# Three load buffers for VectorE's adaLN pieces, with RQ and bt moved into the `mt` ring

## The chip, the cores and the metric

The kernel runs on one core of a Trainium2 chip. The metric is the device time of one execution in microseconds. The engines are TensorE (PE: matmuls, with PEld for its weight loads), VectorE (DVE), ScalarE (ACT), GpSimd (POOL) and SyncE (SP). POOL and SP here mostly issue DMAs.

## The reference: what is computed

Two layers of a diffusion block work on 256 context tokens and 256 latent tokens of width 2048. Each layer makes the adaLN rows (shift, scale, gate) from a conditioning vector, normalises and modulates the tokens, projects them with one wide matrix, runs three mixers on parts of the columns (S5, attention, a bidirectional mLSTM) and projects back. Cut to what matters here:

```python
for layer in range(DEPTH):
    shift, scale, gate = split(silu(c) @ ada_w[layer] + ada_b[layer], 3)       # 2048 x 6144
    xn = rmsnorm(h_lat, norm_w[layer]) * (1 + scale) + shift
    (..., ml_q, ml_k, ml_v, ml_o, ml_g, ml_z) = split_sections(xn @ w_in[layer])
    ya = s5_branch(...); yb = attention_branch(...)
    # mlstm: q, k = silu(depthwise conv of width 3); gates i, f from ml_g
    #   b = cumsum(log_sigmoid(f)); log_d = b_t - b_s + i_s; running max, exp
    yc = mlstm_branch(...)
    h_lat = h_lat + gate * (concat(ya, yb, yc) @ w_out[layer])
```

The context tokens go through the same layers with a conditioning vector of their own.

## The kernel before

All weights are streamed from HBM in chunks of 512 KB (128 x 1024). `wchunk` loads one into `raw` (three buffers, SP's queue); ScalarE rounds it to `hi`, VectorE subtracts to get `lo` (two buffers each). `proj_a` makes one output of 128 channels by 512 tokens in a PSUM tile `pa` from two chunks: 48 matmuls (`hi` by `xh`, `hi` by `xl`, `lo` by `xh`). `proj_b` does the same for outputs that have the tokens on partitions, in `pb`. Both draw on a pool of three PSUM banks, so the fourth `pa` needs the bank of the first. A callback reads the bank when it is full.

TensorE's stream of projections is the backbone of the program. Beside it, generators (`stream`) and the adaLN queue (`ada_step`) are advanced by `pump` after each chunk, at a rate given as a number. The Tile framework then puts each engine's instructions into one fixed order by its priorities and its account of buffers, so a change in buffers can move instructions on every engine.

The adaLN rows of layer 1 are not made on TensorE: VectorE makes them while the mLSTM part of a layer runs. `adv_open(pool, bufs, rate, ids)` opens a queue of pieces. `ada_load` issues the load of a piece (512 KB, from `adt`) on POOL's queue into an `ar` tile, of which there are `bufs`. `adv_piece` reduces a piece against a row tile `cb`: an instruction `aj` (L365) with a small read-out of its sum into `adp`. In layer 0 there are 64 pieces with two `aj` each (128 `aj`, rate ADR = 1.2 a chunk), in layer 1 there are 32 pieces with one each (rate 1.0). Ahead of the first piece `adv_rows` loads 1 MB into `cb` and applies silu in four steps: a tanh on ScalarE into an `mt` tile, L150 on it, and a product into `cb`.

`mt` is a ring of five tiles of 128 x 516 in the mLSTM pool, from which most short-lived tiles of this part are taken. One user is `ml_conv`, which follows each of the projections mk0 to mk3 and mq0 to mq3: ScalarE writes y from `pa` into an `mt` tile, two VectorE instructions (L153, `mt<-pa`) add the shifted taps out of `pa`, then tanh and a product give `mk`. After the second of them the bank is free.

`ml_gates` works on the input and forget gates as a stream, at the time of mk0 to mk3: `ga0` to `ga6` are small tiles for the logarithm of the sigmoid; `li` is a copy of the input gates; TensorE transposes to rows in PSUM (`psr`); VectorE makes `bt` (a cumulative sum, L1021), `RQ` (a difference, its running maximum L1023 and a copy L1024), and TensorE transposes `RQ` back into `psg`.

At the same time attention runs as another stream. For each head block VectorE reduces the scores (`sm`, L949), ScalarE takes the exponential (`g`), VectorE the reciprocal (L953), ScalarE scales `g`, and TensorE transposes it (`psP`) and multiplies by the values (`psO`). Later in the layer the stream `ml_chain` runs the mLSTM's chunk steps (`psm`, `G`, `hacc`) and `ml_final` its output (`psh`).

Of the kernel before, what the change touches and what calls it, by code (L numbers as in the profile page):

```python
# [9 lines left out]
F32 = mybir.dt.float32  # L10
# [35 lines left out]
ADR = 1.2  # L46
# [77 lines left out]
class Kern:  # L124
# [857 lines left out]
    def ml_gates(self, l):  # L982
        mp = self.mp
        GS = self.GS
        sm = lambda q: mp.tile([128, 4, 2, 4], F32, tag=f"ga{q}", bufs=1, name=self.nm("ga"))
        f, ab, y, u, ln, e = (sm(q) for q in range(6))
        self.V.tensor_copy(f, GS[:, :, :, 1])
        self.ts(ab, f, -1.0, OP.mult)
        self.tt(ab, ab, f, OP.max)
        self.act(y, ab, AF.Exp, scale=-1.0)  # L990
        self.ts(u, y, 1.0, OP.add)
        self.act(ln, u, AF.Ln)
        self.ts(e, u, -1.0, OP.add)
        self.tt(e, y, e, OP.subtract)
        self.V.reciprocal(u, u)
        self.tt(e, e, u, OP.mult)
        self.tt(ln, ln, e, OP.add)
        self.stt(f, f, 0.0, ln, OP.min, OP.subtract)
        li = mp.tile([128, 4, 2, 4], F32, tag="ga6", bufs=1, name=self.nm("ga"))
        self.V.tensor_copy(li, GS[:, :, :, 0])  # L1000
        yield
        rows = self.pA.tile([128, 512], F32, tag="bA", name=self.nm("psr"))
        for w, src in enumerate((li, f)):
            z = []
            for d in range(2):
                zt = mp.tile([128, 4, 2, 4], F32, tag=f"gz{w}{d}", bufs=1, name=self.nm("gz"))
                self.V.memset(zt, 0.0)
                if d == 0:
                    self.V.tensor_copy(zt[:, :, 0], src[:, :, 0])
                else:  # L1010
                    zv = zt.rearrange("p (a b) d h -> p a b d h", b=2)
                    sv = src.rearrange("p (a b) d h -> p a b d h", b=2)
                    self.V.tensor_copy(zv[:, :, 0, 1], sv[:, :, 1, 1])
                    self.V.tensor_copy(zv[:, :, 1, 1], sv[:, :, 0, 1])
                z.append(zt.rearrange("p a d h -> p (a d h)"))
            o = rows[:32, w * 128:w * 128 + 128]
            self.mm(o, z[0], self.c("I"), start=True, stop=False)
            self.mm(o, z[1], self.c("J"), start=False, stop=True)
        RQ = mp.tile([128, 128], F32, tag="RQ", bufs=1, name=self.nm("RQ"))
        bt = mp.tile([128, 128], F32, tag="bt", bufs=1, name=self.nm("bt"))  # L1020
        self.V.tensor_tensor_scan(bt[:32], self.c("ONE")[:32], rows[:32, 128:256], 0.0, op0=OP.mult, op1=OP.add)  # L1021
        self.tt(RQ[0:32], rows[:32, 0:128], bt[:32], OP.subtract)
        self.V.tensor_tensor_scan(RQ[32:64], RQ[0:32], RQ[0:32], -3.0e38, op0=OP.max, op1=OP.max)  # L1023
        self.V.tensor_copy(RQ[64:96], bt[:32])  # L1024
        yield
        pt = self.pA.tile([128, 512], F32, tag="bA", name=self.nm("psg"))
        self.tr(pt[:, 0:96], RQ[0:96], k=96)
        self.tr(pt[:, 128:224], RQ[0:96, 127:128].to_broadcast([96, 128]), k=96)
        TK = mp.tile([128, 12, 2, 4], F32, tag="TK", bufs=1, name=self.nm("TK"))
        self.V.tensor_copy(TK.rearrange("p a d h -> p (a d h)"), pt[:, 0:96])  # L1030
        LB = mp.tile([128, 3, 4, 8], F32, tag="LB", bufs=1, name=self.nm("LB"))
        self.V.tensor_copy(LB.rearrange("p a b c -> p (a b c)"), pt[:, 128:224])
        tr = mp.tile([128, 12, 4], F32, tag="tr", bufs=1, name=self.nm("tr"))
        self.V.tensor_copy(tr, TK[:, :, 1])
        yield
        pf = self.pA.tile([128, 512], F32, tag="bA", name=self.nm("psf"))
        self.mm(pf[:, 0:48], self.c("J"), tr.rearrange("p a h -> p (a h)"))
        self.V.tensor_copy(TK[:, :, 1], pf[:, 0:48].rearrange("p (a h) -> p a h", h=4))
        yield
        q = lambda n: TK[:, 4 * n:4 * n + 4].rearrange("p s d h -> p s (d h)")  # L1040
        a_, cm, b_ = q(0), q(1), q(2)
        t8 = lambda nme: mp.tile([128, 4, 8], F32, tag=nme, bufs=1, name=self.nm(nme))
        ms, ML, M, WIN, GU, W, DEC = (t8(n) for n in ("gms", "gML", "gM", "gWIN", "gGU", "gW", "gDEC"))
        self.V.memset(ms[:, 0], 0.0)
        for s in range(4):
            self.tt(ML[:, s], ms[:, s], LB[:, 1, s], OP.max)
            if s < 3:
                self.tt(ms[:, s + 1], LB[:, 2, s], ML[:, s], OP.add)
        self.tt(M, cm, ms, OP.max)
        self.tt(WIN, ms, M, OP.subtract)  # L1050
        self.act(WIN, WIN, AF.Exp)
        self.tt(GU, b_, M, OP.add)
        self.act(GU, GU, AF.Exp, scale=-1.0)
        self.tt(W, a_, ML, OP.subtract)
        self.act(W, W, AF.Exp)
        self.ts(W, W, 128.0 ** -0.5, OP.mult)
        self.tt(DEC, ms, ML, OP.subtract)
        self.act(DEC, DEC, AF.Exp)
        self.mg = dict(a=a_, M=M, WIN=WIN, GU=GU, W=W, DEC=DEC)
# [173 lines left out]
    def layer(self, l, sp):  # L1233
# [71 lines left out]
        mpg = tc.tile_pool(name=f"ml{l}", bufs=1, side="left", reuse_waits="tile")  # L1305
        mp = self.mp = mpg.__enter__()
        if need:
            self.adv_open(mp, 2, ADR, range(0, 64))
        else:
            self.adv_open(mp, 2, 1.0, range(64, 96))  # L1310
        self.msk = mp.tile([128, 2, 128], F32, tag="msk", bufs=1, name=self.nm("msk"))
        nc.sync.dma_start(self.msk.rearrange("p d t -> p (d t)"), self.i["mask"])
        self.ml_conv_w(l)
# [285 lines left out]
```

## Time and profile before

| | |
|---|---|
| median of 3 runs | 1673.41 us (1667.14 to 1675.38) |
| the profiled execution | 1667.69 us |
| its span | 1665.9 us |
| PE busy in it | 1588.9 us (95%) |
| DVE busy | 1203.8 us (72%) |
| ACT busy | 669.6 us (40%) |
| POOL busy | 131.6 us (8%) |
| mean granted clock of TensorE | 0.988 of full speed |

The span is the time from the first to the last instruction of the profiled execution; that execution's own time is 1.8 us longer. Busy times are sums over the span; an engine's wait matters where an engine that sets the end waits for it. Rows of the profile name an instruction by its line, engine, operation and tiles, `out<-in`.

### The profile page before, as it was taken

Reading aid. Unit: us, or ns where it says so; the run is one execution under the profiler, and the core shown is the slowest. Engines: PE = TensorE matmul, PEld = TensorE weight load, DVE = VectorE, ACT = ScalarE, POOL = GpSimd, SP = SyncE. Lnnn points to the kernel's source line nnn. Section 1 sums busy time; section 2 is a strip of 40 time slices with the busy share of each in tenths; the row PEclk is TensorE's granted clock in tenths of the full one; section 3 lists DMA queues with packets and bytes.
Section 4 is the critical chain, followed back from the end, with each engine's and each line's share of the span. In section 5 each row is a group of like instructions: output and inputs, shape, how many; then the busy total and the mean of one; then the engine's idle time right before and its main releaser. Section 6 shows DMA issues by size and latency. Waiting matters only on the chain.

```text
span 1665.9 us, 27067 instructions
## 1 busy us (share of the span) xinstructions
PE 1588.9 (95%) x10542; PEld 1346.6 (81%) x10542; DVE 1203.8 (72%) x2545; ACT 669.6 (40%) x1278; POOL 131.6 (8%) x252
## 2 busy tenths in 40 slices
PE   5999999999999999999999999899999999999996
PEld 1567988878778868788887777689999879999996
DVE  5432888777949796899899887446787577557744
ACT  3333344434354344322242332553455543254542
POOL 2221000010001110111000110100000011000000
PEclk9999999999999999999999999899999999999998
DMA  9885344351235665565364555524655457653753
GB/s 373 297 304 173 88 143 163 127 181 59 69 104 167 192 187 172 192 202 178 114 211 142 206 181 169 173 88 153 196 157 168 155 183 247 203 165 114 217 179 123
DMA packets 88032, 288.06 MB, mean 173 GB/s; under 512 B 10208, under 2 KB 18144, under 8 KB 87264
## 3 DMA queue, kind: packets, MB, share of 16 engines
q1 hardware_dynamic: 52704, 158.33, 29.2%
q0 software_dynamic: 35200, 128.01, 23.3%
q8 instruction: 82, 1.34, 0.3%
q14 instruction: 46, 0.38, 0.1%
HBM read 268.44 MB, written 17.86 MB: 172 GB/s over the span
## 4 chain that ended last, share of the span: by engine, by line
PE 42%; issue 29%; DVE 13%; DMA 12%; POOL 2%; ACT 1%; POOLq 0%; DVEq 0%; ACTq 0%
PE pa L159 25%; DMA ar<-adt 7%; DMA ar<-ada 4%; PE pb L159 4%; DVE lo L145 3%; PE pu L159 3%; DVE aj L365 2%; POOL ar L284 2%; PE psm L159 2%; PE psY L159 1%; PE psG L159 1%; DVE tp L145 1%; PE psO L159 1%; DVE S L782 1%; PE psS L159 1%
## 5 line engine op out<-in xcount | busy, mean ns | idle before, releaser
L156 ACT ACTIVATE hi<-raw 128x1024 fp32r<-128x1024 f32 x256 | 271.0, 1058 | 554.8 <-PE pa L159 311.6
L159 PE MATMUL pa<-xh,hi 128*128 128x512 f32 (+1 forms) x1408 | 490.5, 348 | 0.0
L159 PE MATMUL pa<-xh,lo 128*128 128x512 f32 (+1 forms) x1408 | 484.9, 345 | 0.7 <-DVE lo L145 0.7
L159 PE MATMUL pa<-xl,hi 128*128 128x512 f32 (+1 forms) x1408 | 484.7, 344 | 0.4 <-DVE xl L145 0.4
L145 DVE TENSOR_TENSOR lo<-raw,hi 128x1024 fp32r<-128x1024 f32 x256 | 312.5, 1221 | 138.2 <-ACT hi L156 131.1
L159 PEld LDWEIGHTS pa<-xh,hi 128*128 128x128 f32 x1408 | 267.2, 190 | 34.7 <-issue 4.5
L159 PEld LDWEIGHTS pa<-xh,lo 128*128 128x128 f32 x1408 | 267.3, 190 | 32.2 <-issue 1.9
L159 PEld LDWEIGHTS pa<-xl,hi 128*128 128x128 f32 x1408 | 267.4, 190 | 31.4 <-issue 2.7
L159 PE MATMUL pb<-lo,xh 128*128 128x256 f32 x832 | 238.5, 287 | 6.1 <-DVE lo L145 6.1
L159 PE MATMUL pb<-hi,xh 128*128 128x256 f32 x832 | 241.7, 290 | 0.0
L159 PE MATMUL pb<-hi,xl 128*128 128x256 f32 x832 | 237.2, 285 | 0.0
L365 DVE CUSTOM_DVE_ANT_0 aj<-ar,cb 128x1024 bf16<-128x1024 f32 x160 | 195.2, 1220 | 47.1 <-DMA ar<-adt 46.1
L159 PEld LDWEIGHTS pb<-lo,xh 128*128 128x128 f32 x832 | 160.3, 193 | 8.7 <-DVE lo L145 7.4
L159 PEld LDWEIGHTS pb<-hi,xh 128*128 128x128 f32 x832 | 160.1, 192 | 5.9 <-issue 5.6
L159 PEld LDWEIGHTS pb<-hi,xl 128*128 128x128 f32 x832 | 160.0, 192 | 1.7 <-issue 1.7
L284 POOL DMA_DIRECT2D ar<-adt x96 | 50.8, 529 | 563.8 <-DVE adp L365 260.1
L159 PE MATMUL adps<-ar,cact 128*2 128x256 f32 x768 | 66.7, 396 | 19.3 <-DVE cact L145 12.8
L284 POOL DMA_DIRECT2D ar<-ada x96 | 50.8, 531 | 315.7 <-PE adps L159 307.4
L159 PE MATMUL pu<-hi,xh 128*128 128x512 f32 x128 | 55.9, 437 | 5.3 <-ACT xh L156 5.3
L156 ACT ACTIVATE g<-psS,sm 128x512 f32<-128x512 f32 (+1 forms) x48 | 29.3, 611 | 64.7 <-DVE sm L149 64.2
L159 PE MATMUL pu<-lo,xh 128*128 128x512 f32 x128 | 54.1, 422 | 0.0
L159 PE MATMUL pu<-hi,xl 128*128 128x512 f32 x128 | 53.4, 425 | 0.0
(301 smaller groups left out, 2153.9 us busy)
## 6 DMA issues: line engine op xcount, KB each, us to landing
raw<-wa SPq DMA_DIRECT2D x112, 512.0 KB, 3.6
ar<-ada POOLq DMA_DIRECT2D x96, 512.0 KB, 5.0
ar<-adt POOLq DMA_DIRECT2D x96, 512.0 KB, 4.0
raw<-wb SPq DMA_DIRECT2D x64, 512.0 KB, 4.0
raw<-wo SPq DMA_DIRECT2D x64, 512.0 KB, 3.6
raw<-wu SPq DMA_DIRECT2D x16, 512.0 KB, 4.2
h<-ht SPq DMA_DIRECT2D x32, 256.0 KB, 5.0
tb<-E POOLq DMA_DIRECT2D x8, 516.0 KB, 3.2
```

The lines of the kernel that those rows point to most:

```text
L145: return self.V.tensor_tensor(o, a, b, op=op)
L156: return self.S.activation(o, a, f, **kw)
L159: return self.T.matmul(o, w, x, start=start, stop=stop, skip_group_check=True)
L284: self.nc.gpsimd.dma_start(raw, self.i[self.aq["src"]][pid])
L365: self.V.tensor_tensor_reduce(junk, raw, row, 1.0, 0.0, OP.mult, OP.add, self.adp[:, half, kind, dt, v:v + 1])
L782: V.tensor_tensor_scan(f(S[:, ri]), f(dt), f(Z[:, ri]), 0.0, op0=OP.mult, op1=OP.add)
```

## The change

The third number of buffers is for `ar`, in both layers. A buffer of it takes 4,096 bytes per partition. The tiles that no longer have memory of their own, `RQ` and `bt` (512 bytes each) and `ga6` (128 bytes), make 1,152 bytes per partition; `RQ` and `bt` are taken from the `mt` ring, and `li` takes the place of `ga1` (`ab`), which is dead by then.

```diff
@@ ml_gates
-        li = mp.tile([128, 4, 2, 4], F32, tag="ga6", bufs=1, name=self.nm("ga"))
+        li = mp.tile([128, 4, 2, 4], F32, tag="ga1", bufs=1, name=self.nm("ga"))
...
-        RQ = mp.tile([128, 128], F32, tag="RQ", bufs=1, name=self.nm("RQ"))
-        bt = mp.tile([128, 128], F32, tag="bt", bufs=1, name=self.nm("bt"))
+        RQ = self.mt(128)
+        bt = self.mt(128)
@@ the mixers of a layer
         if need:
-            self.adv_open(mp, 2, ADR, range(0, 64))
+            self.adv_open(mp, 3, ADR, range(0, 64))
         else:
-            self.adv_open(mp, 2, 1.0, range(64, 96))
+            self.adv_open(mp, 3, 1.0, range(64, 96))
```

The change moves instructions. The first place is on VectorE in layer 0, where the conv of mk0 is (the numbers behind names are counters, and move by two with the change; pa_4616 of before is pa_4618 of after, the output of mk0). Before, from the subtraction that makes RQ on:

```order
L145 TENSOR_TENSOR RQ_4754<-psr_4735,bt_4755 32x128
L150 TENSOR_SCALAR mt_4649<-mt_4649 128x512
L1023 SCALAR_TENSOR_TENSOR RQ_4754<-RQ_4754 32x128
L145 TENSOR_TENSOR cb_4647<-cb_4647,mt_4649 128x512
L150 TENSOR_SCALAR mt_4653<-mt_4653 128x512
L145 TENSOR_TENSOR lo_5013<-raw_5010,hi_5012 128x1024
L145 TENSOR_TENSOR cb_4647<-cb_4647,mt_4653 128x512
L153 SCALAR_TENSOR_TENSOR mt_4760<-pa_4616,cw_4613,mt_4760 128x2x255
L150 TENSOR_SCALAR mt_4657<-mt_4657 128x512
L153 SCALAR_TENSOR_TENSOR mt_4760<-pa_4616,cw_4613,mt_4760 128x2x255
L145 TENSOR_TENSOR cb_4647<-cb_4647,mt_4657 128x512
L150 TENSOR_SCALAR mt_4661<-mt_4661 128x512
```

After the change, from the second `aj` on (the four `cb` rows, a `lo`, the first `aj` and the scan of `bt` stand ahead of these rows):

```order
L365 ISA aj_4669,adp_4606<-ar_4607,cb_4649 128x1024
L365 ISA adp_4606 128x1
L145 TENSOR_TENSOR lo_5069<-raw_5066,hi_5068 128x1024
L365 ISA aj_4723,adp_4606<-ar_4609,cb_4649 128x1024
L365 ISA adp_4606 128x1
L145 TENSOR_TENSOR mt_4756<-psr_4737,mt_4757 32x128
L365 ISA aj_4725,adp_4606<-ar_4609,cb_4649 128x1024
L365 ISA adp_4606 128x1
L153 SCALAR_TENSOR_TENSOR mt_4762<-pa_4618,cw_4615,mt_4762 128x2x255
L1023 SCALAR_TENSOR_TENSOR mt_4756<-mt_4756 32x128
L153 SCALAR_TENSOR_TENSOR mt_4762<-pa_4618,cw_4615,mt_4762 128x2x255
L1024 COPY mt_4756<-mt_4757 32x128
```

Both conv instructions of mk0 (`mt<-pa`) stood ahead of the first `aj`, between the second and the third `cb` row; now they stand behind the fourth `cb` row, the second `lo`, and four `aj`, with the scan of `bt` and the subtraction of `RQ` between these.

The second place is on TensorE at the change from mk2 to mk3 (pa_4889 and pa_5009 of before, pa_4891 and pa_5011 of after; mk3 takes the bank that mk0 had). Before:

```order
L159 MATMUL pa_4889<-xh_1374,lo_4962 128x512
L159 MATMUL pa_5009<-xh_562,hi_5012 128x512
L159 MATMUL pa_5009<-xl_563,hi_5012 128x512
L159 MATMUL pa_5009<-xh_562,lo_5013 128x512
L159 MATMUL pa_5009<-xh_570,hi_5012 128x512
```

After:

```order
L159 MATMUL pa_4891<-xh_1374,lo_4964 128x512
L159 MATMUL pa_5011<-xh_562,hi_5014 128x512
L163 MATMUL psg_4825<-cst,mt_4756 128x96 x2
L159 MATMUL pa_5011<-xl_563,hi_5014 128x512
L159 MATMUL pa_5011<-xh_562,lo_5015 128x512
```

The transposes into `psg` moved up to right behind the first matmul of mk3; before they stood 43 matmuls later.

The third place is on VectorE in the attention of layer 0, at one `lo` and the score reduction behind it (the chunk raw_5881 of before is raw_5883 of after). Before:

```order
L365 ISA aj_5695,adp_4606<-ar_5549,cb_4647 128x1024
L365 ISA adp_4606 128x1
L145 TENSOR_TENSOR lo_5884<-raw_5881,hi_5883 128x1024
L365 ISA aj_5699,adp_4606<-ar_5627,cb_4647 128x1024
L365 ISA adp_4606 128x1
L949 TENSOR_REDUCE sm_5717<-psS_5715 128x1
L365 ISA aj_5701,adp_4606<-ar_5627,cb_4647 128x1024
```

After:

```order
L365 ISA aj_5994,adp_4606<-ar_5881,cb_4649 128x1024
L365 ISA adp_4606 128x1
L365 ISA aj_5996,adp_4606<-ar_5881,cb_4649 128x1024
L365 ISA adp_4606 128x1
L145 TENSOR_TENSOR lo_5886<-raw_5883,hi_5885 128x1024
L949 TENSOR_REDUCE sm_5719<-psS_5717 128x1
L949 TENSOR_REDUCE sm_5728<-psS_5726 128x1
L149 TENSOR_SCALAR sm_5719<-sm_5719 128x1
```

The reduction now follows the `lo` at once, without an `aj` between; ahead of this `lo` stand 36 `aj` of the layer before and 46 after. By the count of the whole order, the reciprocals L953 of the first two softmax blocks of this stretch have 2 more `aj` ahead of them than before, those of the next 7, then 8, and the last 9; from the middle of the layer (64th `aj`) the order of `aj` is that of before up to the 110th, and at the output of the mLSTM (`psh`) three `aj` and one `lo` more stand ahead of `mt` on VectorE, and 19 `pa` matmuls more ahead of `psh` on TensorE. In layer 1 the order changes by a few places.

## Rows read from the trace of the kernel before

**Rows 1.** The page: span, and busy time of each engine.
```profile
span 1665.9 us, 27067 instructions
...
PE 1588.9 (95%) x10542; PEld 1346.6 (81%) x10542; DVE 1203.8 (72%) x2545; ACT 669.6 (40%) x1278; POOL 131.6 (8%) x252
```
**Rows 2.** Waits of PE, 484 to 840 us: total, times, longest, us.
```profile
PE psP L163 <- ACT g L156: 8.5, 7, 1.7
PE psm L159 <- DVE mt L153: 3.4, 1, 3.4
PE psh L163 <- DVE mt L145: 1.4, 1, 1.4
```
**Rows 3.** Waits of PE, 1250 to 1440 us.
```profile
PE pb L159 <- DVE lo L145: 4.7, 2, 2.7
PE psg L163 <- ACT g L156: 1.6, 1, 1.6
```
**Rows 4.** The page, costliest groups: `aj` (busy, mean ns, idle time before).
```profile
L365 DVE CUSTOM_DVE_ANT_0 aj<-ar,cb 128x1024 bf16<-128x1024 f32 x160 | 195.2, 1220 | 47.1 <-DMA ar<-adt 46.1
```
**Rows 5.** The page, DMA issues: loads of the pieces, median us to landing.
```profile
ar<-adt POOLq DMA_DIRECT2D x96, 512.0 KB, 4.0
```
**Rows 6.** Waits of DVE for the pieces, 530 to 569 us.
```profile
DVE aj L365 <- DMA ar<-adt: 7.0, 4, 2.8
```
**Rows 7.** Waits of DVE for the pieces, 530 to 608 us.
```profile
DVE aj L365 <- DMA ar<-adt: 13.7, 8, 2.8
```
**Rows 8.** Waits of DVE for the pieces, 1318 to 1440 us.
```profile
DVE aj L365 <- DMA ar<-adt: 25.6, 20, 2.9
```
**Rows 9.** Timeline of PE at two gaps: start, us, instruction, idle before.
```profile
691.65 0.69 PE L159 MATMUL psm<-v,mt 128*128 128x129 f32 x4 [3.39 <-DVE mt L153]
...
1421.63 0.39 PE L159 MATMUL pb<-lo,xh 128*128 128x256 f32 x1 [2.72 <-DVE lo L145]
```
**Rows 10.** Windows: busy by engine, granted clock, DMA share, GB/s.
```profile
692.00:696.00 4.00, 4.00 (x16) 3.38 (x16) 4.00 (x8) 0.07 (x1) 0.53 (x1) 0.57 0.72 226
1420.00:1424.00 4.00, 2.37 (x15) 2.37 (x15) 2.72 (x5) 0.00 (x0) 1.06 (x2) 0.83 0.45 159
1424.00:1428.00 4.00, 4.00 (x27) 4.00 (x27) 2.96 (x4) 0.00 (x0) 0.53 (x1) 0.74 0.82 268
1428.00:1432.00 4.00, 4.00 (x36) 4.00 (x35) 2.26 (x5) 1.06 (x1) 0.62 (x2) 1.00 0.93 362
```
**Rows 11.** Timeline of DVE around mk0's conv, 493 to 499 us.
```profile
493.34 0.28 DVE L145 TENSOR_TENSOR RQ<-psr,bt 32x128 f32<-32x128 f32 x1
493.55 0.40 DVE L150 TENSOR_SCALAR mt<-mt 128x512 f32<-128x512 f32 x1
493.98 0.41 DVE L1023 TENSOR_TENSOR_SCAN RQ<-RQ 32x128 f32<-32x128 f32 x1
494.43 0.69 DVE L145 TENSOR_TENSOR cb<-cb,mt 128x512 f32<-128x512 f32 x1
...
495.37 1.22 DVE L145 TENSOR_TENSOR lo<-raw,hi 128x1024 fp32r<-128x1024 f32 x1
...
498.10 0.74 DVE L153 SCALAR_TENSOR_TENSOR mt<-pa,cw,mt 128x510 f32<-128x510 f32 x1
```
**Rows 12.** Timeline of ScalarE near 500 us.
```profile
500.14 1.05 ACT L156 ACTIVATE hi<-raw 128x1024 fp32r<-128x1024 f32 x1
```
**Rows 13.** Timeline of PE from mk2's last matmul to mk3's first.
```profile
499.71 0.39 PE L159 MATMUL pa<-xh,lo 128*128 128x512 f32 x1
499.94 0.39 PE L159 MATMUL pa<-xh,hi 128*128 128x512 f32 x1
```
**Rows 14.** Waits of DVE for the pieces, 608 to 700 us.
```profile
DVE aj L365 <- DMA ar<-adt: 5.4, 5, 1.6
```
**Rows 15.** Timeline of DVE ahead of PE's gap at 1421.63.
```profile
1419.21 1.23 DVE L365 CUSTOM_DVE_ANT_0 aj<-ar,cb 128x1024 bf16<-128x1024 f32 x1 [2.59 <-DMA ar<-adt]
...
1420.36 1.22 DVE L145 TENSOR_TENSOR lo<-raw,hi 128x1024 fp32r<-128x1024 f32 x1
```

## Prediction, made before the changed kernel ran

> **What bounds the kernel now.** The page comes first: TensorE (PE) is busy for 1588.9 us of the 1665.9 us span, VectorE (DVE) for 1203.8 [rows 1]. So a transfer that comes sooner, or a DVE instruction that is ready sooner, is worth only the PE gap that it ends. The change touches the two stretches in which VectorE computes layer 1's adaLN rows (`aj` on 512 KB pieces in `ar`): about 484 to 840 us in layer 0 and 1318 to 1440 us in layer 1. The waits of PE in them come next: 8.5 us in seven waits of `psP` for ScalarE's `g` (the softmax; `g` itself waits for DVE's `sm`), 3.4 us in one wait of `psm`, 1.4 us in one of `psh` [rows 2]; in layer 1 4.7 us in two waits of `pb` for `lo` and 1.6 us of `psg` [rows 3]. Together 19.6 us. Then the waits of DVE: `aj` stood 46.1 us behind its loads over the whole kernel [rows 4], although such a load lands 4.0 us after its issue [rows 5]. The two ring buffers are what delays the issue: a buffer is reloaded only when its last `aj` is done. DVE runs in order, so what stands behind the `aj` (`sm`, `lo`, `mt`) is late by the same wait, and then PE. 13.7 us of that wait lie between 530 and 608 us, where the `psP` gaps are, 7.0 of them before 569 [rows 6, 7], and 25.6 us in layer 1 [rows 8].
>
> A long gap costs more than itself. After the 3.39 us before `psm` at 691.65 [rows 9] the granted clock of the next 4 us is 0.57 of full speed; after the 2.72 us before `pb` at 1421.63 it is 0.83 and 0.74 over eight [rows 10]. That is (1 - 0.57) x 4 = 1.7 us and (0.17 + 0.26) x 4 = 1.7 us lost. So the gaps have 19.6 + 3.4 = 23.0 us in them, and this is all that the third buffer can give.
>
> The Trainium skill (Perfetto Trace Analysis, Optimization Strategy) says that a gap which repeats on the engine that should be saturated can mean that the memory for the next tile is short. Here the repeating gap is on DVE, not on PE; taken for DVE's 46.1 us it would promise twice what PE's gaps hold, so the rows decide.
>
> **The memory that pays for it: RQ and bt in the `mt` ring.** The third `ar` buffer needs 4 KB per partition; the change takes its share from `RQ`, `bt` and `li`. `li` reuses a tile of the same shape that is dead by then, and I cost it at nothing: it is one copy on DVE long before. `RQ` and `bt` are now two of the five `mt` buffers, in the midst of the pieces that use them: the four tanh tiles of the `cb` rows and the conv tiles of mk0. The order shows what this does: on DVE the first read of mk0's PSUM bank (`mt<-pa`) stands behind all four `cb` rows, two `lo`, four `aj`, the scan of `bt` and the subtraction of `RQ`. Before, it stood ahead of every `aj`.
>
> Of that place I work out the new time with the durations of before less 0.07 each, since an instruction starts so much ahead of the end of the one before (493.34 + 0.28 = 493.62 against 493.55): L150 0.33, `cb` 0.62, `lo` 1.15, scan 0.34, subtraction 0.21, conv 0.67 [rows 11]; an `aj` 1.22 with its read-out [rows 4]. From 493.3: 4 x 0.33 + 4 x 0.62 + 1.15 = 4.9 gives 498.2. Two `aj` and the scan: 501.0. The next `lo` needs `hi`, done at 500.14 + 1.05 = 501.2 [rows 12], which itself needs mk2's matmuls: 502.3. One `aj`, the subtraction, one `aj`: 505.0. Two conv steps and a scan: 506.8. PE's first matmul of mk3 takes the bank of mk0 (three banks), and before it ran at 499.94 with no gap behind mk2's last at 499.71 [rows 13], because the conv's last read was over at 498.10 + 0.74 = 498.84 [rows 11]. So the cover is 1.1 us and the conv now ends 8.0 us later: a PE stall of 6.9 us. No row shows what follows a 6.9 us gap; the gaps of 2.72 and 3.39 us cost 1.7 us of clock each, the bounds are 0 and twice that, and I take 1.7, since the longer of the two cost no more. Term: **+8.6 us**, where nothing is lost now. `psg` also stands right behind mk3's first matmul and waits for L1024 on DVE, one copy later (0.2 us, inside the rounding).
>
> **The `psP` gaps of layer 0.** DVE now has more `aj` ahead of the same softmax: by the order 2 more ahead of the reciprocals of the first two gaps, 7 more by the third, 8 at the next three and 9 at the last, at 1.22 each [rows 4]: 2.4, 8.5, 9.8 and 11.0 us of work moved ahead. Against it stand the waits that go. If all went, DVE would be later by 8.5 - 7.0 = 1.5 us at the third and 11.0 - 13.7 = -2.7 at the last; if two thirds go (which I take, as a load that shares the queues still lands after 4 us or more), by 3.8 and 1.9. PE itself comes 8.6 us later, so a gap shrinks by what PE is later than DVE. The first two gaps close (PE still 5.9 late), the third closes (4.2), the fourth and fifth close (2.0), and about a fifth of the 8.5 us is left in the last two. So 8.5 - 1.7 = 6.8 us come back: **-6.8**. Bounds: all 8.5, or nothing and more (the third rival).
>
> **The rest of layer 0.** From about 637 to 760 us DVE's order is that of before. The `aj` waits ahead of 691.65 (5.4 us from 608 to 700 [rows 14]) shrink, and the `mt` that `psm` waits for comes by more than the 3.39 us earlier: 3.4 + 1.7 of clock, **-5.1** (bounds 0 and -5.1). At `psh` DVE has three `aj` and a `lo` more ahead (4 x 1.22 = 4.9 us), and PE's `psh` stands 19 matmuls of 0.23 us later, 4.4 us [rows 13]: the 1.4 us stay, 0 (bounds -1.4 and +2).
>
> **Layer 1.** The order changes little here. Each piece feeds one `aj`, and the loads run one behind the other: the `aj` at 1419.21 waited 2.59 us, the `lo` behind it ended at 1421.58, and PE's gap of 2.72 us ended with it [rows 9, 15]. With three buffers a load is out while two pieces wait or are used. DMA engines were at a share of 0.45 in 1420 to 1424 just before DVE's loads came back, and moved 362 GB/s at 0.93 a little later [rows 10], so there is room, not for all. Of 6.3 + 1.7 = 8.0 us I take three quarters: **-6.0** (bounds 0 and -8.0).
>
> **Sum.** +8.6 - 6.8 - 5.1 - 6.0 = -9.3 us: 1667.7 us of the profiled execution (span 1665.9 [rows 1] and 1.8 around it) become 1658.4. That execution is 5.7 us below the median of the three runs, 1673.4; against the median the forecast is **1664 us**.
>
> **The rivals.**
> All gaps go, chance 0.20: every load is there in time, 23.0 us return, the stall costs 6.9 to 8.6: -14.4 to -16.1, so 1657 to 1659. For it: the wait per load is mostly the late issue. Against: landings in this stretch share the queues with the weights, and DVE has 9 `aj` more ahead of the softmax.
>
> Loads bound in layer 1, chance 0.16: the third load only queues behind the two in flight, and the gain of layer 1 is nothing: +8.6 - 6.8 - 5.1 = -3.3, so 1670. For it: 362 GB/s at a share of 0.93 is the highest rate of this stretch [rows 10]. Against: that share is not held, 0.45 stands two windows ahead. The Trainium skill (DMA: Bandwidth & Descriptors, the note on three numbers under Where 436 GB/s comes from) gives about 358 GB/s per core as what HBM binds; by that rule the row is at the ceiling, and the trace agrees with 362.
>
> Slower, chance 0.13: the `aj` that the order pulls ahead are not paid for by earlier loads. Then DVE is later by 8.5 us at the third `psP` gap and 11.0 at the last, PE is dragged to the same lag, 11.0 us, and nothing comes back behind it: 1684. It decides where 11.0 less the removed waits is over 8.4, that is if under 2.6 of the 13.7 us [rows 7] go. For it: the order does pull `aj` ahead of `sm` and `lo`. Against: the loads' own 4.0 us is short beside two pieces of two `aj` each, 4.9 us.
>
> The change does nothing, chance 0.03: the ring is not what holds the issue. The trace speaks against it, POOL's loads wait for `aj`.
>
> **How the numbers follow.** The forecast has the remaining 0.48, with its own range 1660 to 1669 (-13 to -4, from the clock after the stall, one third or all of the waits gone, and half or all of layer 1). A measurement here can tell about 0.5% from no change, that is 8.4 us: faster is under 1665.0, slower over 1681.8. Of the 0.48 about 0.28 lie under 1665; with the first rival 0.48 faster. Slower is most of the third rival and a stall of twice the clock loss: 0.11. The rest, 0.41, is the same. Range 1655 to 1681: under it lies part of the first rival, over it most of the third.
>
> **What would show it.** On PE a gap of about 7 us ahead of mk3's first matmul near 500 us, released by DVE's `mt<-pa`, and the clock lower behind it; without it the ring's term is wrong. The waits of `aj` for `ar<-adt` well under 46.1 us in total; over 30 would make the second or third rival. The `psP` waits under 3 us in total; over 8 us with the `aj` ahead is the third rival. No `psm` gap near 690, and the granted clock there at 1.00. In layer 1 `pb` waiting for `lo` under 1.5 us in total; if DVE still waits there for the loads at shares over 0.9, the second rival. What would make me wrong most: a conv of mk0 that is ready earlier than by my chain, or a place later than 760 us where DVE's pulled `aj` delay PE anew.

## The result and the profile after

The changed kernel takes 1663.83 us (median of 8 runs, 1660.46 to 1666.73); before it is 1673.01 us in the same series. The ratio is 0.9949, 95% interval 0.9935 to 0.9963: 9.2 us less at the medians. In a second series it is 1664.55 us against 1668.58 us, ratio 0.9969 (0.9952 to 0.9985): 4.0 us less. Both intervals lie under 1, so the change is faster, by 0.3 to 0.5%; the prediction speaks of faster from about 0.5% on.

The page of the changed kernel has nearly the engine times of before [rows 1]. What has gone is DVE's wait for the pieces, from 46.1 us [rows 4] to 15.0:

```profile
span 1663.5 us, 27073 instructions
...
PE 1593.0 (96%) x10542; PEld 1350.1 (81%) x10542; DVE 1203.1 (72%) x2545; ACT 668.4 (40%) x1278; POOL 131.2 (8%) x252
...
L365 DVE CUSTOM_DVE_ANT_0 aj<-ar,cb 128x1024 bf16<-128x1024 f32 x160 | 195.1, 1219 | 16.2 <-DMA ar<-adt 15.0
```

The waits of PE in the two stretches, first 484 to 840 us, then 1250 to 1440 us (total, times, longest):

```profile
PE pa L159 <- DVE mt L153: 6.6, 1, 6.6
PE psP L163 <- ACT g L156: 1.3, 1, 1.3
...
PE pb L159 <- DVE lo L145: 3.2, 3, 1.8
PE psg L163 <- ACT g L156: 0.9, 1, 0.9
```

Against [rows 2] and [rows 3] the 8.5 us of `psP` are 1.3, the `psm` and `psh` gaps are gone, and one new wait of 6.6 us stands there: mk3's first matmul, which waits for the conv of mk0. The timeline of PE has it here:

```profile
499.78 0.39 PE L159 MATMUL pa<-xh,lo 128*128 128x512 f32 x1
506.80 0.77 PE L159 MATMUL pa<-xh,hi 128*128 128x512 f32 x1 [6.63 <-DVE mt L153]
```

and the timeline of DVE shows the chain ahead of it (the second conv step ends at 505.90 + 0.75 = 506.65):

```profile
498.27 1.22 DVE L365 CUSTOM_DVE_ANT_0 aj<-ar,cb 128x1024 bf16<-128x1024 f32 x1
...
499.42 0.40 DVE L1021 TENSOR_TENSOR_SCAN mt<-cst,psr 32x128 f32<-32x128 f32 x1
...
501.07 1.23 DVE L145 TENSOR_TENSOR lo<-raw,hi 128x1024 fp32r<-128x1024 f32 x1
...
504.69 0.73 DVE L153 SCALAR_TENSOR_TENSOR mt<-pa,cw,mt 128x510 f32<-128x510 f32 x1
...
505.90 0.75 DVE L153 SCALAR_TENSOR_TENSOR mt<-pa,cw,mt 128x510 f32<-128x510 f32 x1
```

The windows of the changed kernel give the granted clock behind the gap, at the place of the old `psm` gap, and in layer 1 (columns as in [rows 10]):

```profile
506.00:510.00 4.00, 3.20 (x9) 2.57 (x10) 3.94 (x7) 1.30 (x2) 0.00 (x0) 0.50 0.46 136
510.00:514.00 4.00, 4.00 (x14) 3.19 (x13) 3.85 (x13) 2.15 (x5) 0.53 (x1) 0.67 0.42 127
...
692.00:696.00 4.00, 4.00 (x25) 3.55 (x24) 4.00 (x9) 0.00 (x0) 0.53 (x1) 1.00 0.76 258
...
1400.00:1404.00 4.00, 3.95 (x20) 3.95 (x21) 3.04 (x6) 0.00 (x0) 1.05 (x2) 0.57 0.88 281
```

Behind the new gap PE loses 0.50 x 3.2 + 0.33 x 4 = 2.9 us, and the clock near 692 us is full.

To see where the time went, the start of the n-th matmul of PE is compared with that of before. The columns are n, its start before, and how much later it starts in the changed kernel, in a second profile of it, in a second profile of the kernel before, and in the mask-tile version of the experiments:

```
   n   before   change  change-2  before-2  mask tile
3150    446.3    +0.0     +0.3      +0.4      +0.7
3600    530.1    +9.9     +9.3      +0.4      +0.4
4200    638.5    +1.5     +0.0      +0.6      -8.8
5250    856.3    -5.0     -6.6      -0.7     -15.4
6450   1109.0    -0.4     -1.6      +0.5     -15.2
8250   1353.0    -0.4     -1.7      +0.5     -14.9
8850   1446.4    -2.4     +0.7      -0.8     -16.6
```

So in layer 0 the kernel lost 9.9 us at mk3, won 8.4 by 638 us and 6.5 by 856. Then 4.6 us were lost where the change touches nothing, and layer 1 won 2.0. The second profile of the kernel before moves by 1.2 and 1.3 us against the first in these last two stretches, so differences of this size say nothing there.

### The profile page after: what moved, and what is told of

It reads as the page before. It is cut to its first block, busy times and chain, and to the rows that moved or that the text cites. A ratio compares the mean times of both kernels' runs of the same rounds, so it can differ in the third digit from the quotient of the medians.

```text
span 1663.5 us, 27073 instructions
## 1 busy us (share of the span) xinstructions
PE 1593.0 (96%) x10542; PEld 1350.1 (81%) x10542; DVE 1203.1 (72%) x2545; ACT 668.4 (40%) x1278; POOL 131.2 (8%) x252
## 4 chain that ended last, share of the span: by engine, by line
PE 56%; issue 20%; DVE 13%; DMA 8%; ACT 2%; POOL 1%; SPq 0%; DVEq 0%; POOLq 0%; ACTq 0%
PE pa L159 33%; PE pu L159 5%; PE pb L159 4%; DMA ar<-ada 3%; DVE lo L145 3%; DMA ar<-adt 3%; PE psm L159 2%; DVE aj L365 2%; PE psY L159 1%; DMA h<-ht 1%; PE psO L159 1%; PE adps L159 1%; PE psG L159 1%; PE psS L159 1%; DVE S L782 1%
## 5 line engine op out<-in xcount | busy, mean ns | idle before, releaser
L159 PEld LDWEIGHTS pu<-hi,xh 128*128 128x128 f32 x128 | 40.0, 313 | 15.4 <-issue 7.7
```

Of the source, the lines that this page charges most:

```text
L159: return self.T.matmul(o, w, x, start=start, stop=stop, skip_group_check=True)
```

## The experiments

The theory is that of the prediction: the third buffer takes the load waits away and with them PE's gaps, and RQ and bt in the `mt` ring cost a stall by the order on VectorE that comes with them. The main rivals are that the earlier `aj`, not the ring, make the stall, that the lag of PE alone closed the `psP` gaps, and, for layer 1, that the loads' own time is the limit.

**Three buffers without the ring.** RQ and bt take the memory of the mask tile, which is needed only later:

```diff
-        RQ = self.mt(128)
-        bt = self.mt(128)
+        rb = mp.tile([128, 2, 128], F32, tag="msk", bufs=1, name=self.nm("rb"))
+        RQ, bt = rb[:, 0], rb[:, 1]
...
         self.drain(gates)
+        self.msk = mp.tile([128, 2, 128], F32, tag="msk", bufs=1, name=self.nm("msk"))
+        nc.sync.dma_start(self.msk.rearrange("p d t -> p (d t)"), self.i["mask"])
```

Expected:

> Three buffers as in the change, but RQ and bt lie in the memory of the mask tile (its load is moved behind the gates), so the mt ring is that of before. Theory (the ring costs, the third buffer gives): on VectorE mk0's conv stands ahead of every aj again, so no PE gap near 500 us: against the change 6.6 us of wait and about 3 us of lower clock come back, 9.8 us; the psP gaps stay small because the loads come in time. Against before: -8.5 (psP), -5.1 (psm with its clock), -1.4 (psh), -2 (layer 1 as the change showed it) = -17 us, ratio 0.990. Rival (the pulled-ahead aj and the lag of PE, not the loads, closed the psP gaps): without the 9.8 us of lag the psP gaps are back, 4 to 8 us, and the ratio is that of the change, 0.994 to 0.996.

Measured: 1651.66 us, ratio to before 0.9895 (0.9877 to 0.9913). This beats both kernels. Its waits of PE from 484 to 840 us, and of DVE for the pieces there:

```profile
PE psP L163 <- ACT g L156: 0.7, 1, 0.7
PE psg L163 <- ACT g L156: 0.2, 1, 0.2
...
DVE aj L365 <- DMA ar<-adt: 1.2, 1, 1.2
```

There is no gap at mk3, and the `psP` gaps stay closed without the lag. Both halves of the theory hold: by the table layer 0 wins 16.1 us here (from 446 to 856 us), against 5.0 and 6.9 in the change. The rival falls. VectorE's order says more. Ahead of each `lo` of the attention of layer 0 the mask-tile version has at most 3 `aj` more than the kernel before, the changed kernel up to 10 more, and the ring alone (the next run) up to 9 more. So in layer 0 it is the ring, not the third buffer, that pulls most of the `aj` ahead, and the third buffer closes the `psP` gaps with an order close to that of before.

**The ring alone**, with two buffers in both layers:

```diff
-            self.adv_open(mp, 3, ADR, range(0, 64))
+            self.adv_open(mp, 2, ADR, range(0, 64))
...
-            self.adv_open(mp, 3, 1.0, range(64, 96))
+            self.adv_open(mp, 2, 1.0, range(64, 96))
```

> The other half alone: RQ and bt in the mt ring, li on ga1, two buffers in both layers. Theory: the 6.6 us gap at mk3 is there as in the change (VectorE's order has the same four aj ahead of mk0's conv), PE is 9.8 us later from there, some of the psP gaps close against it but the waits for the loads stay (40 us or more in total), the psm gap of 3.4 us and layer 1 stay: +3 to +8 us against before, ratio 1.002 to 1.005. Rival (the stall comes from the third buffer's earlier aj, not from the ring): no gap at mk3, ratio 0.999 to 1.001.

Measured: 1681.34 us, ratio 1.0075 (1.006 to 1.0089). The mechanism holds, the size was too small. The timeline of PE has the same gap at mk3, and one at a `psP`:

```profile
507.36 0.77 PE L159 MATMUL pa<-xh,hi 128*128 128x512 f32 x1 [6.63 <-DVE mt L153]
...
578.18 0.69 PE L163 MATMUL psP<-cst,g 128*128 128x128 f32 x2 [4.20 <-ACT g L156]
```

The second is the mechanism of the prediction's slow rival: `aj` pulled ahead, loads not earlier, PE dragged to DVE's lag. The `psP` waits are fewer (4.8 us in two), but from 530 to 638 us PE wins only 2.1 us, where the change wins 8.4 and 9.3, and over layer 0 it loses 8.5. By its profile another 1.9 us are lost between 856 and 1109 us and 2.5 in layer 1, where VectorE has the `aj` and `lo` in the order of before; why those two are lost was not tested.

**The third buffer in layer 1 only**, as the last but with

```diff
-            self.adv_open(mp, 2, 1.0, range(64, 96))
+            self.adv_open(mp, 3, 1.0, range(64, 96))
```

> As the change, with the third buffer in layer 1 only (layer 0 has two, RQ and bt in the ring in both layers). Theory (layer 1 gives 2 us in the change's profile, since its loads bound it): 2 us under the run with two buffers everywhere. By the prediction's term for layer 1 (6.0 us) it would be 6 us under it. Layer 0 as in that run: gap at mk3, psm gap there.

Measured: 1678.27 us, ratio 1.0058 (1.0037 to 1.008), so about 3 us under the ring alone. The two intervals overlap; the sign and size are those of the smaller term, and the two profiles differ by the same 3.0 us in layer 1.

**A lower rate in layer 1** (1.0 to 0.7 in the same line of the changed kernel):

> The change with the rate of layer 1's pieces at 0.7 a chunk instead of 1.0: the same 32 loads spread over more chunks. Theory (in layer 1 the loads of weights and pieces together are what VectorE waits for): aj waits under 4 us in layer 1 (13.0 in the change), the pb gaps (3.2 us) and the lower clock near 1400 us (1.7) go: 4 to 5 us faster than the change, ratio to before 0.992. Rival (the order of aj and lo on VectorE makes the gap, not the loads): gaps of the same size move to where the aj now are, ratio as the change, 0.995.

Measured: 1663.37 us, ratio 0.9965 (0.9951 to 0.9978). This told nothing of the theory, since the lower rate hardly changed the order: VectorE has the same number of `aj` ahead of every `lo` as in the change, and still waited 15.6 us for pieces in layer 1. As its instructions stand in the order of the change up to 1337 us, the run serves as a third profile of the change up to there.

**Two buffers in layer 1 and three in layer 0**, without the ring:

> The mask-tile version with three buffers in layer 0 and two in layer 1: sizes the term of layer 1 without the ring. Theory: 2 to 3 us slower than the mask-tile version (the difference that the two ring versions with two buffers in layer 0 showed: 1.0075 and 1.0058), ratio 0.991. By the term of the prediction, 6.0 us, it would be 0.993. Layer 0 as in the mask-tile version: no gap at mk3, no psm gap.

Measured: 1655.58 us, ratio 0.9916 (0.9894 to 0.9937), 3.5 us over the mask-tile version by the two ratios, with overlapping intervals; 2.6 us between the starts of the same matmuls at 1338 and 1412 us of the two profiles. Again the smaller term.

**Four buffers in layer 1**, without the ring:

> The mask-tile version with four buffers in layer 1, three in layer 0. Theory (in layer 1 the loads themselves are the limit: pieces and weights share the DMA engines, and a further buffer only lets a load queue): the waits for the pieces stay at 10 us or more in layer 1, the pb gaps at 3 to 5 us, and the time within 1.5 us of the mask-tile version, ratio to before 0.989 to 0.990. Rival (three buffers are still too few): waits under 5 us, no pb gap, 4 us faster, ratio 0.987.

Measured: 1650.29 us, ratio 0.9889 (0.9868 to 0.991). The time is within 1.5 us of three buffers, as the theory had it, but the waits fell further than it allowed. From 1250 to 1440 us, first PE, then DVE:

```profile
PE pb L159 <- DVE lo L145: 3.1, 1, 3.1
PE psg L163 <- ACT g L156: 0.2, 1, 0.2
...
DVE aj L365 <- DMA ar<-adt: 5.8, 5, 1.9
```

One late `lo` is left and costs nearly what three did (4.3 us in the mask-tile version, where DVE waited 14.7 us). In this version 158 of the 160 `aj` stand ahead of that `lo`, in the mask-tile version 155, in the kernel before 149. And with each further buffer the loads themselves are slower: in layer 1 a piece lands 4.0 us after its issue (median) with two buffers, 4.8 with three and 5.6 with four, and the weights of the same stretch (`raw<-wb`) in 4.3, 5.3 and 5.4 us (all without the ring).

**Half the bytes in layer 1**, without the ring:

```diff
-        self.nc.gpsimd.dma_start(raw, self.i[self.aq["src"]][pid])
+        if self.aq["src"] == "adt" and pid >= 64:
+            self.nc.gpsimd.dma_start(raw[:, 0:512], self.i["adt"][pid][:, 0:512])
+        else:
+            self.nc.gpsimd.dma_start(raw, self.i[self.aq["src"]][pid])
...
```

The part that is not shown lets `aj` read the loaded half twice; the kernel leaves out half of the gate row.

> The mask-tile version in which each load of layer 1's pieces moves only the first half of the columns (256 KB instead of 512 KB), and aj reads that half twice: VectorE's work and its order stay, layer 1's gate row is left out in half. Theory (the load time bounds layer 1): waits for pieces under 3 us there, pb gaps under 1 us, no lower clock near 1400 us, 5 to 6 us faster than the mask-tile version, ratio 0.986. Rival (what delays lo is the order on VectorE, aj ahead of it, or the late hi): gaps stay at 3 us or more, ratio 0.9895.

Measured: 1644.43 us, ratio 0.9859 (0.9837 to 0.9881). The same stretch:

```profile
PE pb L159 <- DVE lo L145: 0.7, 1, 0.7
PE psg L163 <- ACT g L156: 0.2, 1, 0.2
...
DVE aj L371 <- DMA ar<-adt: 4.9, 5, 1.5
```

With shorter loads the gaps nearly close: between 1338 and 1412 us PE wins 6.0 us against the mask-tile version. VectorE's work is the same (1.22 us for an `aj`), but its order is not: it is that of the four-buffer version, except for one `aj`. Against that version PE wins 3.8 us in the same stretch, and the medians differ by 5.9 us. A piece lands in 3.2 us here and `raw<-wb` in 4.4. So the loads' own time holds most of what is left in layer 1, as the second rival had it; this run does not separate the time of the pieces from that of the weights beside them.

**One tile in the ring**, bt alone:

```diff
-        RQ, bt = rb[:, 0], rb[:, 1]
+        RQ, bt = rb[:, 0], self.mt(128)
```

> The mask-tile version with bt alone in the mt ring and RQ in the mask tile's memory. On VectorE two aj instead of four then stand ahead of mk0's conv. Theory (the stall is the work that the ring's order puts ahead of the conv): the gap at mk3 is 6.6 less two aj and about one more short row, 3.5 to 4.2 us, plus up to 3 us of lower clock, part of it given back at the psP gaps: 3 to 7 us slower than the mask-tile version, ratio 0.992 to 0.994. Rival (what counts is that RQ waits for a ring buffer, not the place of the conv): no gap, ratio 0.9895.

Measured: 1661.25 us, ratio 0.9957 (0.9941 to 0.9973), about 10 us over the mask-tile version. The timeline of PE:

```profile
504.98 0.77 PE L159 MATMUL pa<-xh,hi 128*128 128x512 f32 x1 [3.73 <-DVE mt L153]
```

The gap is as forecast from the order, so it is the work ahead of the conv that sets it. The total was expected at 3 to 7 us. By the profiles 5.9 us are lost up to 530 us and 1.0 by 638, nothing is given back there since no `psP` gap was there to close, and 1.6 us more are lost between 934 and 1060 us, 1.8 in layer 1. These last two are of the size by which two profiles of one kernel differ.

**Both kernels again**, for second profiles:

> The changed kernel once more, for a second profile. Its first profile gave 5.0 us by 850 us and lost 4.6 of them between 940 and 1075 us, in output projection and the next layer's start, whose instructions the change leaves as they are. Theory (that loss belongs to the execution, not to the change): in this profile the stretch from 850 to 1110 us takes the time that it takes in the kernel before within 2 us, while the gap of 6.6 us at mk3 and the closed psP and psm gaps are there again. Rival (a change in the buffers' places or in the DMA queues costs something there): again 3 us or more lost in that stretch, with the psM wait near 962.

> The kernel before once more, for a second profile: its first profiled execution was 5.3 us under its median of eight runs. Theory (stretches that the change does not touch vary from one execution to the next): the psP, psm, psh, pb and psg gaps of the first profile are there again within 2 us in total, and the execution's time differs from the first by its waits and clock outside 484 to 840 and 1318 to 1440 us. Rival: the gaps in these two stretches themselves vary by 4 us or more, so that the terms of the prediction cannot be read from one profile. Ratio to before 0.999 to 1.001.

The kernel before: 1670.24 us, ratio 1.0001 (0.9984 to 1.0018), its gaps 17.5 us in all against 19.6 in the first profile, each within 1.3 us (`psP` 7.2 us, `psm` 2.5, `psh` 1.3, `pb` 4.4, `psg` 2.1). The terms of layer 0 can thus be read from one profile. Those of layer 1 of the changed kernel cannot: its `pb` waits are 3.2 us in the first profile and 7.2 in the second. The changed kernel lost 5.0 us in the untouched stretch, as the rival had it. Timelines of PE there, of before, of the change, of the change again, and of the run with the lower rate, whose order there is that of the change:

```profile
966.08 0.73 PE L163 MATMUL psM<-cst,KW 128*128 128x128 f32 x3 [0.37 <-ACT KW L156]
```

```profile
962.54 0.73 PE L163 MATMUL psM<-cst,KW 128*128 128x128 f32 x3 [1.69 <-ACT KW L156]
```

```profile
962.08 0.90 PE L163 MATMUL psM<-cst,KW 128*128 128x128 f32 x3 [2.88 <-ACT KW L156]
```

```profile
964.73 0.73 PE L163 MATMUL psM<-cst,KW 128*128 128x128 f32 x3 [0.67 <-ACT KW L156]
```

This wait is the end of a chain that begins 15 us earlier, at a transfer of the S5 tables (`tb<-E`). Its issue is as much earlier as all the rest, at 947.60 us before, 942.72 and 941.10 in the change, but VectorE, which clears E next, waits longer for it. Timelines of DVE, in the same order:

```profile
951.66 0.07 DVE L689 MEMSET E<- 128x8 f32 x1 [0.19 <-DMA tb<-E]
```

```profile
947.66 0.07 DVE L689 MEMSET E<- 128x8 f32 x1 [1.09 <-DMA tb<-E]
```

```profile
946.58 0.07 DVE L689 MEMSET E<- 128x8 f32 x1 [1.62 <-DMA tb<-E]
```

```profile
950.78 0.07 DVE L689 MEMSET E<- 128x8 f32 x1 [0.98 <-DMA tb<-E]
```

From its issue to that row it takes 4.1, 4.9, 5.5 and 4.8 us, and what follows adds the rest; behind PE's gaps of 1.69 and 2.88 us the granted clock is 0.65 and 0.61 from 962 to 966 us. In the lower-rate run it stays at 1.00 behind the gap, and the stretch loses 1.4 us, about as much as the second profile of before (1.2). So of three executions with the same order two lose 4.6 and 5.0 us and one does not, and neither the theory nor the rival is shown. Nor is the long transfer enough: with one tile in the ring it took 5.3 us and with four buffers 5.5, and the stretch lost 1.7 and 1.8 us. In the mask-tile version it took 4.6 us and the stretch lost 0.1 us, with the ring alone 5.0 and 1.9. What makes the loss large in two executions stays open.

## Why the prediction was right, and where it was not

The forecast of 1664 us and the median of 1663.83 agree, and the direction and the two mechanisms are shown. The sum is closer than its terms deserve.

**The stall.** Forecast: 6.9 us of gap and 1.7 of clock, 8.6. Measured: 6.6 of gap and 2.9 of clock in the first profile; by the starts of PE's matmuls 9.9 us in all, and 9.1 in the second profile. The chain on DVE was right to 0.2 us (conv over at 506.65, forecast 506.8). The ring alone shows the same 6.63 us, one tile in it 3.73 and none in it no gap, so the cause is shown. The clock term was too small: I took the value of shorter gaps.

**The `psP` gaps.** Forecast -6.8; -8.4 and -9.3 between 530 and 638 us. More than two thirds of the waits went: DVE's wait for pieces in layer 0 is 2.0 us where it was 20.5. The prediction set the `aj` that are pulled ahead against the loads that come sooner; the runs show that the first come mostly with the ring and the second with the buffer.

**The rest of layer 0.** Forecast -5.1; -6.5 and -6.6. The `psm` gap and its clock loss are gone, as said, and `psh`, which I left at 1.4 us, closed too.

**Layer 1.** Forecast -6.0; -2.0 and +2.4 in the two profiles, some -3 by the two pairs of versions that differ in nothing else. This is the step that failed: "there is room, not for all ... I take three quarters". I read the room from one window with a share of 0.45; in layer 1 of the changed kernel the DMA engines also have windows in which they are busy throughout, as here (columns as in [rows 10]):

```profile
1368.00:1372.00 4.00, 4.00 (x18) 2.97 (x16) 2.99 (x12) 0.75 (x5) 1.05 (x2) 1.00 1.00 386
```

"The order changes little here" was wrong too. Ahead of the `lo` at 1420.36 [rows 15] stood 154 `aj`; with three buffers all 160 do, and ahead of the ten others between 1360 and 1433 us 1 to 6 more than before. With two buffers (the ring alone) the counts are those of before, so here it is the third buffer that moves them. VectorE's waits for pieces did fall by half (25.6 [rows 8] to 13.0 us, 15.7 in the second profile), but the last wait, ahead of a `lo`, moved instead of going. In the second profile an `aj` ahead of that `lo` waits 3.85 us for its piece, and PE waits for the `lo`:

```profile
1419.49 1.22 DVE L365 CUSTOM_DVE_ANT_0 aj<-ar,cb 128x1024 bf16<-128x1024 f32 x1 [3.85 <-DMA ar<-adt]
...
1422.35 0.49 PE L159 MATMUL pb<-lo,xh 128*128 128x256 f32 x1 [3.42 <-DVE lo L145]
```

With half the bytes 0.73 us of gap are left. The second rival, which I gave 0.16, was right for most of layer 1; no run has three buffers with the order of before, so what the order alone costs there is open. The 1.7 us of clock in this term are not fixed either: in the second profile of before the same gap left the granted clock at 1.00.

```profile
1422.33 0.39 PE L159 MATMUL pb<-lo,xh 128*128 128x256 f32 x1 [2.86 <-DVE lo L145]
...
1424.00:1428.00 4.00, 4.00 (x36) 4.00 (x35) 2.37 (x3) 0.00 (x0) 0.77 (x2) 1.00 0.79 315
```

The Trainium skill (DMA: Bandwidth & Descriptors, the note on three numbers) has about 358 GB/s as the limit of HBM for one core. The window above, at 386 GB/s, lies over that figure, so it is not the ceiling of this run, and the 362 GB/s of [rows 10] do not show one either. The run with half the bytes, whose highest window of 4 us in layer 1 has 271 GB/s, fits a limit by bytes.

**Outside the stretches.** Forecast 0; +4.6 and +5.0 between 856 and 1109 us, +1.4 in the lower-rate run with the same order, +1.2 in the second profile of before. No part of the prediction looked there, and the cause stays open. Together with layer 1 this makes the profiled execution of the change only 2.5 us shorter than that of before, where the sum said 9.3. The medians differ by 9.2 us: the profiled executions of before lie 5.3 and 3.4 us under their medians, those of the change 1.4 and 3.8 us over theirs. What the timed executions do otherwise is not in the traces. In the second series the medians differ by 4.0 us only. So that the total is met is partly luck.

## What to carry to other kernels

A buffer is bought with memory, and what it is bought with has a price of its own: look at who waits in the ring that two more tiles enter, and what the static order then puts ahead of a read that frees a PSUM bank. Here the same buffer paid for with memory that lay idle (a constant loaded too early) was worth 9 to 12 us more by the ratios. In a stretch where loads are already dense, a deeper ring moves the late transfer rather than removing it: the loads land later, and the order puts more of the work that waits for them ahead of what the main engine needs. Fewer bytes did what a fourth buffer did not.

## What the runs showed of the hardware

TensorE's granted clock after a single gap: after 6.63 us in the changed kernel it was 0.50 (the lower of its two levels, 1.2 of 2.4 GHz) and then 0.67 in the next two windows of 4 us, and after 1.82 us at 1400.05 it was 0.57. In the stretches with the pieces the `psP` gaps of up to 1.7 us before [rows 2] left it at 1.00 in the windows around them. Between these sizes the length did not decide it: the 1.69 us at 962.54 were followed by 0.65, the 2.86 us at 1422.33 in the second profile of before by 1.00.

With more loads of 512 KB in flight beside the weights, each landed later: 4.0, 4.8 and 5.6 us (median) with two, three and four buffers, and 3.2 us at half the size.

One transfer in a stretch that the change does not touch held VectorE until 4.0 to 5.5 us after its issue in different executions; the longest wait of PE behind it was 2.9 us.
